# Gate and up projections of an FFN in one pass, two of eight k pairs with seven block products instead of eight

## The chip, the cores and the metric

The kernel runs on one core of a Trainium2 chip. The metric is the device time of one launch in microseconds, as the median over runs; the kernel before takes 2212.3 us (three runs, 2211.59 to 2212.45).

TensorE (PE) multiplies and adds up into PSUM; its weight loads are shown apart as PEld. VectorE is DVE, ScalarE is ACT, GpSimd is POOL, and SyncE (SP) issues the loads of weights from HBM.

## The reference, cut to what matters

Two residual layers on 256 tokens of width 2048: a mixer, then a dense SwiGLU FFN of inner width 5632, twice, then a final RMSNorm. The change touches the two FFNs alone.

```python
D_MODEL, SEQ, DEPTH = 2048, 256, 2
D_FF = 5632

def swiglu(x, wg, wu, wd):
    return (jax.nn.silu(x @ wg) * (x @ wu)) @ wd
...
h = h + swiglu(rms_norm(h, ffn_norm[layer]), ffn_w_gate[layer], ffn_w_up[layer], ffn_w_down[layer])
```

## The kernel before

All weights are float32 and each is used once. A product in float32 precision is made of three passes: a value is split into a rounded part `hi` (by ACT, `AF.Copy` into float32r) and the rest `lo` (by DVE, a subtraction), and `x @ w` becomes `xh@wh + xl@wh + xh@wl`. Activations are split once per layer, weights as they arrive.

**Streaming the weights.** `order` (L285) lists all weight blocks in the order of use. `load_next` (L71) issues the next 512 KB tile `w` (128 partitions x 1024) on SP's queue, into one of four buffers (`WBUFS`). `split_next` (L92) takes the oldest loaded tile, makes `wh` (ACT, L102) and `wl` (DVE, L103) of it, in one of three buffers each, puts its two halves (512 columns, one k tile each) on the list `pend`, and calls `load_next`, whose DMA must wait until the `w` tile four back has been read. `quarter` (L114) calls `fill`, which splits tiles until more than `ahead` = 3 halves are pending, lets delayed work run (`tick`), and hands out the oldest half.

**The FFN** (`ffn`, L431). The inner width is 11 blocks of 512 columns, in two groups (`HALVES`: 6 and 5 blocks). For each block `gemm_tok` (L200) makes the gate product in two PSUM banks (one for each 128 tokens): 16 k tiles, for each of them six matmuls 128x128 by 128x512. ACT reads it out with SiLU (`sg`, L444). Then `gemm_tok` makes the up product in two further banks, which DVE reads out and multiplies (`ac`, L449). Three quarters later (`self.later(3, turn)`) `turn` transposes `ac` on PE (L463, eight 128x128 transposes into two `sm` banks) and splits it into `hh` and `hl` (L166, L167). After a group's blocks, its down projection (L478) runs over `HX` for four blocks of output columns.

So a block of gate and up is 2 x 16 x 6 = 192 matmuls, 16 weight tiles and 8 transposes; there are 22 such blocks in the two FFNs. PSUM has four `mm` banks (gate and up of a block, used in turn) and four `sm` banks (transposes and small sums).

The order on each engine is set by the tile framework's scheduler, which may move independent instructions past each other; instructions on one engine run in that order, and each waits for semaphores of others.

Of the kernel before, what the change touches and what calls it, by code (L numbers as in the profile page):

```python
# [18 lines left out]
P = 128  # L19
T = 256  # L20
# [10 lines left out]
WBUFS = 4  # L31
WARM = 10
EARLY = 4
HALVES = ((0, 6), (6, NFB))
XPOS, APOS, SPOS = [(0, 1), (1, 0), (1, 2)], [(2, 0), (2, 1)], 1
GAPS = dict(
# [16 lines left out]
class Trunk:  # L53
# [17 lines left out]
    def load_next(self):  # L71

        if not self.blocks:
            return
        src = self.blocks[0]
# [11 lines left out]
        self.loaded.append(w)  # L87
        self.half = 0 if end else 1
        if end:
            self.blocks.pop(0)  # L90

    def split_next(self):  # L92

        nc = self.nc
        w = self.loaded.pop(0)
# [12 lines left out]
        self.load_next()  # L108

    def fill(self):  # L110
        while len(self.pend) <= self.ahead and self.loaded:
# [173 lines left out]
    def order(self):  # L285
        a, b = self.a, []
# [26 lines left out]
    def build(self):  # L313
        tc, nc, a = self.tc, self.nc, self.a
        self.ahead, self.half, self.early = 3, 0, EARLY
        self.blocks, self.loaded, self.pend = self.order(), [], []
        self.delayed, self.lane, self.wait = [], [], 0
        with (
            tc.tile_pool(name="const", bufs=1) as cp,
            tc.tile_pool(name="xs", bufs=4) as self.xs,  # L320
# [17 lines left out]
            with tc.tile_pool(name="even", bufs=1) as self.tp:  # L338
                X, ssq = self.even_mix()
            with tc.tile_pool(name="ff0", bufs=1) as self.tp:  # L340
                X, ssq = self.ffn(X, ssq, "g_od", self.rope_tables)
                rs = self.rstd_tok(ssq)
            with tc.tile_pool(name="odd", bufs=1) as self.tp:
                X, ssq = self.odd_mix(X, rs)
            with tc.tile_pool(name="ff1", bufs=1) as self.tp:
# [82 lines left out]
        nc.scalar.activation(rb, ps[:, :T], AF.Copy)  # L428


    def ffn(self, X, ssq, gname, between=None):  # L431
        nc = self.nc
        rs = self.rstd_tok(ssq)
        new_ssq = self.xs.tile([P, 2, 4], F32, tag="ssq", name="ssq", bufs=2)
        for half, (b0, b1) in enumerate(HALVES):
            HX = []
            if half and between:
                between()
            for b in range(b0, b1):
                pg = self.gemm_tok(X, range(4))  # L440
                sg, ac = [], []
                for t in range(2):
                    s = self.tp.tile([P, 512], F32, tag="sg", name="sg", bufs=2)
                    nc.scalar.activation(s, pg[t], AF.Silu, scale=rs[:, t : t + 1])  # L444
                    sg.append(s)
                pu = self.gemm_tok(X, range(4))
                for t in range(2):
                    s = self.tp.tile([P, 512], F32, tag="ac", name="ac", bufs=2)
                    nc.vector.scalar_tensor_tensor(  # L449
                        out=s, in0=pu[t], scalar=rs[:, t : t + 1], in1=sg[t],  # L450
                        op0=ALU.mult, op1=ALU.mult,
                    )
                    ac.append(s)
                hh = self.tp.tile([P, 4, T], F32R, tag="hh", name="hh", bufs=6)
                hl = self.tp.tile([P, 4, T], F32R, tag="hl", name="hl", bufs=6)
                HX += [(hh[:, j], hl[:, j]) for j in range(4)]
# [1041 lines left out]
```

## Time and profile before

| | |
|---|---|
| median of three runs | 2212.3 us |
| profiled execution: its own time, its span | 2212.2 us, 2210.4 us |
| PE busy | 2192.0 us, 99% of the span |
| DVE busy | 1291.7 us, 58% |
| ACT busy | 1051.7 us, 48% |
| DMA | mean 183 GB/s; 57.6% of 16 engines on the weight queue |

The profile is one execution. A busy PE counts overlapping matmuls (each row lasts some 390 ns while the next begins sooner), so its share says that PE is never without work, and the time of a matmul is to be read from the distance of starts. In the waits, ACT waits for PE to free a buffer and DVE waits for ACT: both are ahead of PE.

### The profile page before, as it was taken

The page shows a single profiled execution, that of the slowest core. Times are in us where ns is not written, and L with a number is a line of the kernel's source. Part 1 is how long each engine was busy: PE and PEld are TensorE (multiplying, and loading weights), DVE is VectorE, ACT ScalarE, POOL GpSimd, SP SyncE. Part 2 cuts the span into 40 slices and gives each one's busy share as a digit, 9 for nine tenths or more (in the row PEclk, how much of TensorE's full clock was granted, in tenths as well). Part 3 has the DMA queues.
Part 4 walks back from the last instruction along what each step waited for, and adds up shares of the span by engine and source line. Part 5 has one row for each costly group of instructions (what it writes and reads, how often), then busy time and mean ns, then how long its engine had stood idle before and what let it go on. Part 6 is the DMA issues. An engine that isn't in the chain of part 4 may idle for free.

```text
span 2210.4 us, 29062 instructions
## 1 busy us (share of the span) xinstructions
PE 2192.0 (99%) x11278; PEld 1826.9 (83%) x11278; DVE 1291.7 (58%) x1782; ACT 1051.7 (48%) x1435; POOL 30.0 (1%) x41
## 2 busy tenths in 40 slices
PE   9999999999999999999999999999999999999998
PEld 8888888778888888888888888888888888888886
DVE  6886688476454444444555688564454454444554
ACT  7755564464444433444444545454444433444443
POOL 0000100000000000000000000000000000000000
PEclk9999999999999999999999999999999999999999
DMA  8466347446666665666665554466665666666664
GB/s 294 143 187 181 120 144 227 144 136 200 190 189 189 190 193 192 191 190 191 190 188 185 179 162 143 150 201 189 190 190 188 190 194 193 192 191 190 188 191 154
DMA packets 124650, 405.14 MB, mean 183 GB/s; under 512 B 24896, under 2 KB 25152, under 8 KB 124128
## 3 DMA queue, kind: packets, MB, share of 16 engines
q1 hardware_dynamic: 122896, 398.31, 57.6%
q0 software_dynamic: 896, 3.80, 0.5%
q8 instruction: 88, 1.44, 0.3%
q10 hardware_dynamic: 720, 1.18, 0.1%
q14 instruction: 50, 0.41, 0.0%
HBM read 400.10 MB, written 3.15 MB: 182 GB/s over the span
## 4 chain that ended last, share of the span: by engine, by line
PE 92%; DVE 3%; ACT 2%; issue 1%; DMA 0%; POOLq 0%; POOL 0%; SPq 0%; DVEq 0%
PE mm L59 87%; PE sm L59 4%; DVE wl L103 1%; PE sm L463 1%; ACT wh L102 1%; PE sm L225 0%; DMA dN<-DG 0%; ACT DG L789 0%; DMA Nb<-dN 0%; PE sm L1303 0%; ACT TT L793 0%; DVE h L757 0%; DVE G L782 0%; ACT G L794 0%; DVE h L756 0%
## 5 line engine op out<-in xcount | busy, mean ns | idle before, releaser
L103 DVE TENSOR_TENSOR wl<-w,wh 128x1024 fp32r<-128x1024 f32 (+1 forms) x745 | 907.4, 1218 | 795.4 <-ACT wh L102 793.5
L102 ACT ACTIVATE wh<-w 128x1024 fp32r<-128x1024 f32 (+1 forms) x745 | 786.1, 1056 | 1001.9 <-PE mm L59 948.7
L59 PE MATMUL mm<-wh,x 128*128 128x512 f32 x3328 | 897.8, 391 | 0.9 <-DVE x L167 0.6
L59 PEld LDWEIGHTS mm<-wh,x 128*128 128x128 f32 x3328 | 620.3, 188 | 128.9 <-DVE x L167 0.9
L59 PE MATMUL mm<-wl,x 128*128 128x512 f32 x1664 | 513.6, 390 | 0.7 <-DVE wl L103 0.7
L59 PEld LDWEIGHTS mm<-wl,x 128*128 128x128 f32 x1664 | 312.2, 188 | 66.4 <-DVE wl L103 1.1
L59 PE MATMUL mm<-x,wh 128*128 128x512 f32 x992 | 357.4, 402 | 1.6 <-ACT wh L102 1.6
L59 PE MATMUL mm<-x,wl 128*128 128x256 f32 x992 | 279.7, 282 | 0.6 <-DVE wl L103 0.6
L59 PE MATMUL mm<-wh,hh 128*128 128x512 f32 x704 | 274.5, 390 | 0.0
L59 PE MATMUL mm<-wh,hl 128*128 128x512 f32 x704 | 273.9, 389 | 0.0
L59 PEld LDWEIGHTS mm<-x,wh 128*128 128x128 f32 x992 | 186.8, 188 | 45.2 <-ACT wh L102 1.8
L59 PE MATMUL mm<-wl,hh 128*128 128x512 f32 x704 | 220.1, 389 | 0.0
L59 PEld LDWEIGHTS mm<-x,wl 128*128 128x128 f32 x992 | 188.1, 190 | 2.0 <-DVE wl L103 1.6
L59 PEld LDWEIGHTS mm<-wl,hh 128*128 128x128 f32 x704 | 132.2, 188 | 27.4
L59 PEld LDWEIGHTS mm<-wh,hl 128*128 128x128 f32 x704 | 132.2, 188 | 27.3
L59 PEld LDWEIGHTS mm<-wh,hh 128*128 128x128 f32 x704 | 132.2, 188 | 27.1
L59 PE MATMUL mm<-l,wh 128*128 128x512 f32 x120 | 44.0, 404 | 0.0
L255 DVE TENSOR_TENSOR h<-mm,h 128x512 f32<-128x512 f32 x54 | 34.7, 685 | 11.6 <-PE mm L59 11.6
L449 DVE SCALAR_TENSOR_TENSOR ac<-mm,rstd,sg 128x512 f32<-128x512 f32 x44 | 31.0, 746 | 14.0 <-PE mm L59 14.0
L59 PE MATMUL mm<-l,wl 128*128 128x256 f32 x120 | 34.5, 288 | 0.0
L167 DVE TENSOR_TENSOR hl<-sm,hh 128x512 fp32r<-128x512 f32 x44 | 28.2, 682 | 0.0
L169 ACT ACTIVATE x<-sm,pkt 128x256 fp32r<-128x256 f32 x52 | 22.4, 470 | 10.8 <-DVE x L170 9.8
(260 smaller groups left out, 1078.4 us busy)
## 6 DMA issues: line engine op xcount, KB each, us to landing
w<-f_gate SPq DMA_DIRECT2D x176, 512.0 KB, 4.4
w<-f_up SPq DMA_DIRECT2D x176, 512.0 KB, 3.8
w<-f_down SPq DMA_DIRECT2D x176, 512.0 KB, 4.4
w<-e_in SPq DMA_DIRECT2D x94, 512.0 KB, 4.3
w<-e_out SPq DMA_DIRECT2D x32, 512.0 KB, 4.4
w<-o_out SPq DMA_DIRECT2D x32, 512.0 KB, 3.7
w<-o_in SPq DMA_DIRECT2D x26, 512.0 KB, 3.8
w<-e_in SPq DMA_DIRECT2D x16, 256.0 KB, 6.1
```

The lines of the kernel that those rows point to most:

```text
L59: return self.nc.tensor.matmul(out, lhsT, rhs, start=start, stop=stop, skip_group_check=shared)
L102: nc.scalar.activation(hi[:, sl], w[:, sl], AF.Copy)
L103: nc.vector.tensor_tensor(out=lo[:, sl], in0=w[:, sl], in1=hi[:, sl].bitcast(F32), op=ALU.subtract)
L167: nc.vector.tensor_tensor(out=lo, in0=src, in1=hi.bitcast(F32), op=ALU.subtract)
L169: nc.scalar.activation(hi, src, AF.Copy, scale=scale)
L255: nc.vector.tensor_tensor(out=hs, in0=ps[t], in1=hs, op=ALU.add)
L449: nc.vector.scalar_tensor_tensor(out=s, in0=pu[t], scalar=rs[:, t : t + 1], in1=sg[t], op0=ALU.mult, op1=ALU.mult,)
L463: nc.tensor.transpose(pt[:, i * T + t * P : i * T + t * P + P], ac[t][:, (j + i) * P : (j + i + 1) * P], self.ident,)
```

## The change

**Order of the products.** Gate and up of a block are made in one pass over k (`gate_up`) instead of one after the other, in four `mm` banks `c[n][t]` (n is gate or up, t the half of the tokens). k is taken in eight pairs of k tiles. In six pairs, each pair is one gate tile and one up tile of 1024 columns, as now, and takes eight block products of three matmuls, 24 matmuls.

**Seven products.** In pairs 3 and 7 (`SPAIRS`) the 2x2 block product (two token halves x two k tiles, by two k tiles x gate and up) is made by Strassen's algorithm in Winograd's form: seven products of three matmuls (`triple`), 21 matmuls for 24. One each goes to `c[0][0]`, `c[1][0]` and `c[0][1]`, and four into the `sm` banks `q[0]` to `q[3]`, which add up over both pairs.

**Sums of blocks.** Products need sums of blocks. On the side of the activations `x_sums` makes four sums for each of the two pairs once per FFN (DVE, and one split). On the side of the weights `split_pair` makes, for each such pair of tiles, four differences of 512 columns (DVE), and splits them in two steps of 1024 (ACT and DVE), beside the split of one block `b22`; the second half of the up tile is not split as it stands. The gate tile `w` is held until then, and its `load_next` is called together with that of the up tile.

**Reading out.** At a block's end ACT copies the four `mm` banks and `q[0]` to SBUF, and DVE makes eight sums and two products, with two SiLU on ACT between them (before: two SiLU and two products). `turn` comes nine quarters later (`TURN`) instead of three.

Nothing else is changed: the same bytes are loaded, and the mixers, down projections and the end are as they were.

```diff
+TURN = 9
+SPAIRS = (3, 7)
...
         hi = self.wp.tile([P, 1024], F32R, tag="wh", name="wh", bufs=3)
         lo = self.wp.tile([P, 1024], F32R, tag="wl", name="wl", bufs=3)
+        if role == "up":
+            self.split_pair(self.held, w, hi[:, 0:512], lo[:, 0:512])
+            self.load_next()
+            self.load_next()
+            return
...
-        self.load_next()
+        if role == "gate":
+            self.held = w
+        else:
+            self.load_next()
+
+    def split_pair(self, wg, wu, hi, lo):
+
+        V = self.nc.vector
+        b11, b21, b12, b22 = wg[:, 0:512], wg[:, 512:], wu[:, 0:512], wu[:, 512:]
+        self.split((hi, lo), b22)
+        t = self.tp.tile([P, 4, 512], F32, tag="o", name="t", bufs=self.tbufs)
+        th = self.tp.tile([P, 4, 512], F32R, tag="th", name="th")
+        tl = self.tp.tile([P, 4, 512], F32R, tag="tl", name="tl")
+        for o, x, y in (
+            (t[:, 0], b12, b11), (t[:, 1], b22, t[:, 0]), (t[:, 3], b21, t[:, 1]),
+            (t[:, 2], b22, b12),
+        ):
+            V.tensor_tensor(out=o, in0=x, in1=y, op=ALU.subtract)
+        for i in (2, 0):
+            self.split((th[:, i : i + 2], tl[:, i : i + 2]), t[:, i : i + 2])
+        self.pend.append(((hi, lo), *((th[:, i], tl[:, i]) for i in range(4))))
...
-                    r += [a["f_gate"][l, n, kc] for kc in range(4)]
-                    r += [a["f_up"][l, n, kc] for kc in range(4)]
+                    for p in range(8):
+                        cs = slice(p % 2 * 1024, p % 2 * 1024 + 1024)
+                        wg, wu = (a[k][l, n, p // 2][:, cs] for k in ("f_gate", "f_up"))
+                        r += [("gate", wg), ("up", wu)] if p in SPAIRS else [wg, wu]
...
+    def triple(self, out, x, w, start, stop):
+        self.mm(out, x[0], w[0], start, False)
+        self.mm(out, x[1], w[0], False, False)
+        self.mm(out, x[0], w[1], False, stop)
...
+        a11, a21, a12, a22 = x[:, 0, 0], x[:, 0, 1], x[:, 1, 0], x[:, 1, 1]
+        s = self.tp.tile([P, 4, P], F32, tag="e3", name="s")
+        V.tensor_tensor(out=s[:, 0], in0=a21, in1=a22, op=ALU.add)
+        V.tensor_tensor(out=s[:, 1], in0=s[:, 0], in1=a11, op=ALU.subtract)
+        V.tensor_tensor(out=s[:, 2], in0=a11, in1=a21, op=ALU.subtract)
+        V.tensor_tensor(out=s[:, 3], in0=a12, in1=s[:, 1], op=ALU.subtract)
+        self.split(dst, s)
...
+        c = [[self.ps("mm") for _ in range(2)] for _ in range(2)]
+        q = None
+        for p in range(8):
+            k = 2 * p
+            if p not in SPAIRS:
+                for n in range(2):
+                    for j in range(2):
+                        w = self.quarter()
+                        for t in range(2):
+                            end = n == 1 and t == 1 and j == 1 and p == LASTP
+                            self.triple(c[n][t], x(k + j, t), w, k + j == 0, end)
+                continue
+            b11, b21 = self.quarter(), self.quarter()
+            b22, t1, t2, t3, t4 = self.quarter()
+            new, end = q is None, p == SPAIRS[-1]
+            q = q or [self.ps() for _ in range(4)]
+            sh, sl = sums[p]
+            s1, s2, s3, s4 = ((sh[:, i], sl[:, i]) for i in range(4))
+            self.triple(c[0][0], x(k + 1, 0), b21, False, end)
+            self.triple(c[1][0], s4, b22, False, end)
+            self.triple(c[0][1], x(k + 1, 1), t4, False, end)
+            self.triple(q[0], x(k, 0), b11, new, end)
+            self.triple(q[1], s2, t2, new, end)
+            self.triple(q[2], s3, t3, new, end)
+            self.triple(q[3], s1, t1, new, end)
...
+        for o, i in ((u[1], c[1][1]), (g[0], c[0][0]), (u[0], c[1][0]), (g[1], c[0][1])):
+            S.activation(o, i, AF.Copy)
+        S.activation(u2, q[0], AF.Copy)
+        add(g[0], q[0], g[0])
+        S.activation(g[0], g[0], AF.Silu, scale=rs[:, 0:1])
+        add(u2, q[1], u2)
+        add(u3, q[2], u2)
+        add(g[1], g[1], u3)
+        S.activation(g[1], g[1], AF.Silu, scale=rs[:, 1:2])
+        for t, y in ((0, u2), (1, u3)):
+            add(u[t], q[3], u[t])
+            add(u[t], u[t], y)
+        for t in range(2):
+            V.scalar_tensor_tensor(
+                out=u[t], in0=u[t], scalar=rs[:, t : t + 1], in1=g[t],
+                op0=ALU.mult, op1=ALU.mult,
...
+            self.later(6 + 2 * i, lambda p=p: self.x_sums(X0, p, sums[p]))
...
-                pg = self.gemm_tok(X, range(4))
-                sg, ac = [], []
-                for t in range(2):
-                    s = self.tp.tile([P, 512], F32, tag="sg", name="sg", bufs=2)
-                    nc.scalar.activation(s, pg[t], AF.Silu, scale=rs[:, t : t + 1])
-                    sg.append(s)
-                pu = self.gemm_tok(X, range(4))
...
+                ac = self.gate_up(X, sums, rs)
...
-                self.later(3, turn)
+                self.later(TURN, turn)
```

Where the instructions stand, at the end of the third block of the first FFN and in the fourth. **DVE at the block's end, before**: the two products that read out the up banks (`ac`), two weight splits, and the splits of the transposed block (`hl`).

```order
L103 TENSOR_TENSOR wl_5967<-w_5898,wh_5966 128x1024
L103 TENSOR_TENSOR wl_5985<-w_5916,wh_5984 128x1024
L449 SCALAR_TENSOR_TENSOR ac_5996<-mm_5850,rstd_5045,sg_5846 128x512
L449 SCALAR_TENSOR_TENSOR ac_5998<-mm_5851,rstd_5045,sg_5848 128x512
L103 TENSOR_TENSOR wl_6011<-w_5934,wh_6010 128x1024
L103 TENSOR_TENSOR wl_6043<-w_5952,wh_6042 128x1024
L167 TENSOR_TENSOR hl_6001<-sm_6022,hh_6000 128x512
L167 TENSOR_TENSOR hl_6001<-sm_6029,hh_6000 128x512
L103 TENSOR_TENSOR wl_6061<-w_5970,wh_6060 128x1024
```

**DVE at the same place, after**: `eg`, `eu`, `eq`, `e3` are the SBUF tiles of the read-out, `sm` the four banks `q`; the `wl` rows are splits of tiles of the next block, the first two of its pair 0, then those of pair 1.

```order
L522 TENSOR_TENSOR eg0_6106<-sm_5929,eg0_6106 128x512
L522 TENSOR_TENSOR eq_6110<-sm_5930,eq_6110 128x512
L522 TENSOR_TENSOR eu0_6108<-sm_5932,eu0_6108 128x512
L522 TENSOR_TENSOR e3_6111<-sm_5931,eq_6110 128x512
L522 TENSOR_TENSOR eu0_6108<-eu0_6108,eq_6110 128x512
L522 TENSOR_TENSOR eg1_6107<-eg1_6107,e3_6111 128x512
L522 TENSOR_TENSOR eu1_6109<-sm_5932,eu1_6109 128x512
L536 SCALAR_TENSOR_TENSOR eu0_6108<-eu0_6108,rstd_5045,eg0_6106 128x512
L522 TENSOR_TENSOR eu1_6109<-eu1_6109,e3_6111 128x512
L113 TENSOR_TENSOR wl_6142<-w_6063,wh_6141 128x1024
L536 SCALAR_TENSOR_TENSOR eu1_6109<-eu1_6109,rstd_5045,eg1_6107 128x512
L113 TENSOR_TENSOR wl_6160<-w_6065,wh_6159 128x1024
```

Ten instructions of the read-out stand ahead of the second split of the next block's pair 1 (`wl_6160`), where two stood.

**DVE at pair 3 of that next block, after**: `t` holds the four differences, `tl` their `lo` parts, `wl_6244` is that of `b22`, `w_6145` and `w_6163` are the gate and the up tile of pair 3.

```order
L135 TENSOR_TENSOR t_6247<-w_6163,w_6145 128x512
L113 TENSOR_TENSOR wl_6228<-w_6145,wh_6227 128x1024
L197 TENSOR_TENSOR hl_6130<-sm_6207,hh_6129 128x512
L197 TENSOR_TENSOR hl_6130<-sm_6214,hh_6129 128x512
L135 TENSOR_TENSOR t_6247<-w_6163,t_6247 128x512
L197 TENSOR_TENSOR wl_6244<-w_6163,wh_6243 128x512
L135 TENSOR_TENSOR t_6247<-w_6145,t_6247 128x512
L135 TENSOR_TENSOR t_6247<-w_6163 128x512
L197 TENSOR_TENSOR tl_6249<-t_6247,th_6248 128x1024
L113 TENSOR_TENSOR wl_6269<-w_6181,wh_6268 128x1024
L197 TENSOR_TENSOR tl_6249<-t_6247,th_6248 128x1024
```

The first row needs the up tile `w_6163`, and the other rows stand behind it. The buffer of that tile is the one that `wl_6160` above reads, four tiles back. Before, a pair of tiles was two `wl` rows.

**PE in a block, before**: two banks in turn, `wh` twice and `wl` once for each; here from one k tile to the next.

```order
L59 MATMUL mm_5370<-wl_5379,x_4812 128x512
L59 MATMUL mm_5371<-wl_5379,x_4812 128x512
L59 MATMUL mm_5370<-wh_5410,x_4812 128x512 x2
L59 MATMUL mm_5371<-wh_5410,x_4812 128x512 x2
L59 MATMUL mm_5370<-wl_5411,x_4812 128x512
L59 MATMUL mm_5371<-wl_5411,x_4812 128x512
```

**PE at pair 3 of the next block, after**: `sh3` and `sl3` are the sums of activations, `th` and `tl` the split differences; two matmuls with `wh_6227` stand just ahead.

```order
L62 MATMUL mm_6131<-wl_6228,x_4812 128x512
L62 MATMUL mm_6133<-wh_6243,sh3_5049 128x512
L62 MATMUL mm_6133<-wh_6243,sl3_5050 128x512
L62 MATMUL mm_6133<-wl_6244,sh3_5049 128x512
L62 MATMUL sm_6280<-wh_6227,x_4812 128x512 x2
L62 MATMUL sm_6280<-wl_6228,x_4812 128x512
L62 MATMUL mm_6132<-th_6248,x_4812 128x512 x2
L62 MATMUL sm_6281<-th_6248,sh3_5049 128x512
L62 MATMUL sm_6281<-th_6248,sl3_5050 128x512
L62 MATMUL sm_6281<-tl_6249,sh3_5049 128x512
L62 MATMUL sm_6282<-th_6248,sh3_5049 128x512
L62 MATMUL mm_6132<-tl_6249,x_4812 128x512
```

The last row is the third matmul of the product with the fourth difference; it stands behind fifteen matmuls of the pair (the two just ahead and the thirteen here), and five more follow it. Each waits on what DVE and ACT make for this pair; before, only on `wh` and `wl`.

## Rows read from the trace of the kernel before

**Rows 1.** The page: span, and busy time of each engine.

```profile
span 2210.4 us, 29062 instructions
PE 2192.0 (99%) x11278; PEld 1826.9 (83%) x11278; DVE 1291.7 (58%) x1782; ACT 1051.7 (48%) x1435; POOL 30.0 (1%) x41
```

**Rows 2.** The chain of work, 470 to 560 us: start us, us, what.

```profile
483.69 43.54 PE mm L59 x192
527.23 0.87 PE sm L463 x8
528.10 31.98 PE mm L59 x141
```

**Rows 3.** PE's timeline in a block: start us, us, engine, line, operation, out<-in, count.

```profile
597.76 0.62 PE L59 MATMUL mm<-wl,x 128*128 128x512 f32 x2
598.21 1.07 PE L59 MATMUL mm<-wh,x 128*128 128x512 f32 x4
599.12 0.62 PE L59 MATMUL mm<-wl,x 128*128 128x512 f32 x2
599.57 1.07 PE L59 MATMUL mm<-wh,x 128*128 128x512 f32 x4
```

**Rows 4.** Waits of the run: who for whom, us in total, times, longest us.

```profile
ACT wh L102 <- PE mm L59: 948.7, 615, 4.2
DVE wl L103 <- ACT wh L102: 793.5, 574, 4.8
```

**Rows 5.** Groups by shape: busy us, mean ns of one, idle before.

```profile
L103 DVE TENSOR_TENSOR wl<-w,wh 128x1024 fp32r<-128x1024 f32 x737 | 902.0, 1224 | 794.2 <-ACT wh L102 792.3 <-PE sm L59 0.8 <-PE mm L59 0.5
L102 ACT ACTIVATE wh<-w 128x1024 fp32r<-128x1024 f32 x737 | 781.2, 1060 | 1000.6 <-PE mm L59 948.7 <-issue 35.3 <-DMA w<-e_out 4.0
L255 DVE TENSOR_TENSOR h<-mm,h 128x512 f32<-128x512 f32 x54 | 34.7, 685 | 11.6 <-PE mm L59 11.6
L449 DVE SCALAR_TENSOR_TENSOR ac<-mm,rstd,sg 128x512 f32<-128x512 f32 x44 | 31.0, 746 | 14.0 <-PE mm L59 14.0
L444 ACT ACTIVATE sg<-mm,rstd 128x512 f32<-128x512 f32 x44 | 27.5, 674 | 0.0
L167 DVE TENSOR_TENSOR x<-mix,x 128x512 fp32r<-128x512 f32 x7 | 4.8, 684 | 0.1
L769 ACT ACTIVATE BKt<-sm 128x512 f32<-128x512 f32 x8 | 4.7, 588 | 3.2 <-PE sm L766 3.2
```

**Rows 6.** Busy time in stretches: us, PE, PEld, DVE, ACT, POOL, PEclk, DMA share, GB/s.

```profile
482.00:526.00 44.00, 44.00 (x200) 36.53 (x199) 35.01 (x66) 22.02 (x27) 2.35 (x2) 1.00 0.62 187
526.00:570.00 44.00, 44.00 (x200) 36.53 (x199) 21.80 (x20) 19.11 (x20) 0.00 (x0) 1.00 0.62 190
1474.00:1518.00 44.00, 44.00 (x200) 36.54 (x199) 22.31 (x24) 22.02 (x27) 1.30 (x2) 1.00 0.65 214
```

**Rows 7.** DVE's timeline around a read-out, columns as in 3.

```profile
613.14 1.41 DVE L449 SCALAR_TENSOR_TENSOR ac<-mm,rstd,sg 128x512 f32<-128x512 f32 x2 [0.63 <-PE mm L59]
614.47 1.22 DVE L103 TENSOR_TENSOR wl<-w,wh 128x1024 fp32r<-128x1024 f32 x1
616.73 1.23 DVE L103 TENSOR_TENSOR wl<-w,wh 128x1024 fp32r<-128x1024 f32 x1 [1.04 <-ACT wh L102]
617.87 1.28 DVE L167 TENSOR_TENSOR hl<-sm,hh 128x512 fp32r<-128x512 f32 x2
```

**Rows 8.** ACT's timeline around a read-out.

```profile
546.74 1.06 ACT L102 ACTIVATE wh<-w 128x1024 fp32r<-128x1024 f32 x1 [1.66 <-PE mm L59]
547.71 1.25 ACT L444 ACTIVATE sg<-mm,rstd 128x512 f32<-128x512 f32 x2
549.46 1.06 ACT L102 ACTIVATE wh<-w 128x1024 fp32r<-128x1024 f32 x1 [0.51 <-PE mm L59]
```

**Rows 9.** The page's DMA issues: line, operation, count, KB each, us to landing.

```profile
w<-f_gate SPq DMA_DIRECT2D x176, 512.0 KB, 4.4
w<-f_up SPq DMA_DIRECT2D x176, 512.0 KB, 3.8
```

More of the change, by code (lines that the diff above doesn't have):

```diff
@@ L33 @@
 EARLY = 4
+TURN = 9
+SPAIRS = (3, 7)
+LASTP = max(p for p in range(8) if p not in SPAIRS)
 HALVES = ((0, 6), (6, NFB))
@@ L74, in load_next @@
             return
-        src = self.blocks[0]
+        src, role = self.blocks[0], None
+        if isinstance(src, tuple):
+            role, src = src
         w = self.wp.tile([P, 1024], F32, tag="w", name="w", bufs=WBUFS)
@@ L86, in load_next @@
             end = o + 1024 == src.shape[-1]
-        self.loaded.append(w)
+        self.loaded.append((w, role))
         self.half = 0 if end else 1
@@ L94, in split_next @@
         nc = self.nc
-        w = self.loaded.pop(0)
+        w, role = self.loaded.pop(0)
         hi = self.wp.tile([P, 1024], F32R, tag="wh", name="wh", bufs=3)
         lo = self.wp.tile([P, 1024], F32R, tag="wl", name="wl", bufs=3)
+        if role == "up":
[3 more added lines that the diff above has]
+            return
         n = 512 if self.early else 1024
@@ L317, in build @@
         self.delayed, self.lane, self.wait = [], [], 0
+        self.tbufs = 1
         with (
@@ L344, in build @@
                 X, ssq = self.odd_mix(X, rs)
+            self.tbufs = 2
             with tc.tile_pool(name="ff1", bufs=1) as self.tp:
@@ L428, in row_bcast, with x_sums @@
         nc.scalar.activation(rb, ps[:, :T], AF.Copy)
+    def triple(self, out, x, w, start, stop):
+        self.mm(out, x[0], w[0], start, False)
+        self.mm(out, x[1], w[0], False, False)
+        self.mm(out, x[0], w[1], False, stop)
+    def x_sums(self, X, p, dst):
+        V = self.nc.vector
+        x = self.tp.tile([P, 2, 2, P], F32, tag="eq", name="x")
+        for j in range(2):
+            xh, xl = X[2 * p + j][:2]
+            V.tensor_tensor(
+                out=x[:, j].rearrange("p t n -> p (t n)"), in0=xh.bitcast(F32),
+                in1=xl.bitcast(F32), op=ALU.add,
+            )
+        a11, a21, a12, a22 = x[:, 0, 0], x[:, 0, 1], x[:, 1, 0], x[:, 1, 1]
[5 more added lines that the diff above has]
+        self.split(dst, s)
@@ new lines, in gate_up @@
+    def gate_up(self, X, sums, rs):
+        nc, V, S = self.nc, self.nc.vector, self.nc.scalar
+        half = (slice(0, P), slice(P, T))
+        x = lambda k, t: (X[k][0][:, half[t]], X[k][1][:, half[t]])
+        c = [[self.ps("mm") for _ in range(2)] for _ in range(2)]
[4 more added lines that the diff above has]
+                for n in range(2):
+                    for j in range(2):
+                        w = self.quarter()
[16 more added lines that the diff above has]
+            self.triple(q[3], s1, t1, new, end)
+        e = lambda tag: self.tp.tile([P, 512], F32, tag=tag, name=tag)
+        g = [e("eg0"), e("eg1")]
+        u = [e("eu0"), e("eu1")]
+        u2, u3 = e("eq"), e("e3")
+        add = lambda o, i0, i1: V.tensor_tensor(out=o, in0=i0, in1=i1, op=ALU.add)
+        for o, i in ((u[1], c[1][1]), (g[0], c[0][0]), (u[0], c[1][0]), (g[1], c[0][1])):
[14 more added lines that the diff above has]
+                op0=ALU.mult, op1=ALU.mult,
+            )
+        return u
@@ L433, in ffn @@
         rs = self.rstd_tok(ssq)
+        sums = {}
+        for i, p in enumerate(SPAIRS):
+            sums[p] = tuple(
+                self.tp.tile([P, 4, P], F32R, tag=f"s{n}{p}", name=f"s{n}{p}") for n in "hl"
+            )
+            self.later(6 + 2 * i, lambda p=p: self.x_sums(X0, p, sums[p]))
+        X0 = X
         new_ssq = self.xs.tile([P, 2, 4], F32, tag="ssq", name="ssq", bufs=2)
@@ L439, in ffn @@
             for b in range(b0, b1):
-                pg = self.gemm_tok(X, range(4))
-                sg, ac = [], []
-                for t in range(2):
-                    s = self.tp.tile([P, 512], F32, tag="sg", name="sg", bufs=2)
-                    nc.scalar.activation(s, pg[t], AF.Silu, scale=rs[:, t : t + 1])
-                    sg.append(s)
-                pu = self.gemm_tok(X, range(4))
[L447 to L453, printed above, removed]
+                ac = self.gate_up(X, sums, rs)
                 hh = self.tp.tile([P, 4, T], F32R, tag="hh", name="hh", bufs=6)
```

## The prediction

> **What bounds the kernel now.** The page says that PE is busy for 99% of the span while DVE is at 58% and ACT at 48% [rows 1]. That share alone does not say that a matmul less saves its time, so the chain of work comes next: through a block of gate and up it is PE alone, 192 matmuls of line 59 in 43.54 us and the eight transposes in 0.87 us, with nothing between [rows 2]. So a matmul costs 43.54/192 = 0.2268 us; the timeline has the same distance (eight starts from 597.76 to 599.57, 0.226 apart) [rows 3], while a row itself lasts longer, as matmuls overlap. The waits show who has room: ACT waits for PE to free a buffer, DVE for ACT [rows 4]. In a block DVE works 21.8 of 44 us and ACT 19.1 [rows 6]. PE's order sets the end, and DVE and ACT are a few tiles ahead of it.
>
> **What is removed.** A pair with seven products has 21 matmuls for 24. Two pairs a block and 22 blocks take away 2 x 3 x 22 = 132 matmuls of 0.2268 us, 29.9 us. All of it lies on the path. A block then has 186 matmuls, 42.18 us, and with the transposes 43.05.
>
> **What DVE and ACT get.** In front of a pair with seven products stood one split of the up tile (1.22 us on DVE); now five instructions of 512 columns (0.684) and two of 1024 (1.224), 5.87 us, so 4.65 more, 9.3 a block. The read-out was two products of 0.746; now it is eight sums of 0.685 and the two products, 5.5 more [rows 5]. DVE goes from 21.8 to 36.6 us in 43.05. ACT gets two splits of 1.06 and one of 0.62 for one of 1.06 (3.4 a block, 0.62 by the longer form of 512 columns) and five copies of 0.588 [rows 5], and goes from 19.1 to some 25.4. Neither becomes the bound on the average. But DVE's work is bunched: the read-out at a block's end, and the eleven rows at pair 3.
>
> **How fast DVE gets through a bunch** decides. A DVE instruction that waits for nothing starts before the one ahead has ended: `wl` starts at 616.73, lasts 1.23, and `hl` starts at 617.87, 0.09 earlier than that end; the two `hl` together take 1.28 [rows 7], where one is 0.68. So in a bunch 1024 columns cost 1.14, 512 columns 0.60, and the product with a scalar 0.66 (two in 1.41) [rows 7]. ACT likewise: a split starts at 546.74 and the next instruction at 547.71, 0.97 later, and two SiLU take 1.25 [rows 8], so 0.97 for 1024 columns and 0.49 for a copy of 512.
>
> The Trainium skill (VectorE: DVE Perf Modes, § The DRAIN you can't avoid) says that the next operation does not start until the pipe of the one before is empty, and that chaining cannot skip this; its next section lets an instruction that isn't held start earlier. Here the trace speaks for the second: 0.08 to 0.09 us of overlap wherever nothing is waited for. By the first the sum would be that of the third rival below.
>
> **The chain through one block.** I count from the first matmul of a block, at 0.
> ACT can split the block's first tile when the tiles of the former pair 6 are free, at the start of pair 7: -21 x 0.2268 = -4.76. Then in its row come a split, a copy, a split and four copies, 0.97 + 0.49 + 0.97 + 3 x 0.49 + 0.59 = 4.49, so the copy that DVE's first sum needs ends at -0.27, and DVE starts at about -0.2.
> DVE goes through the rows up to `wl_6160`: eight sums at 0.60, a product 0.66, `wl_6142` 1.14, a product 0.66, `wl_6160` 1.22: 8.48, to 8.3. This frees the buffer for the up tile of pair 3.
> Its load lands 3.8 us later by the row of `f_up`, 4.4 by that of `f_gate` [rows 9]. I take the middle, 4.1, since both loads run on one queue and here come in closer succession than the 2.72 us between two splits now [rows 8]. It lands at 12.4.
> DVE then does its rows at pair 3: 0.60, 1.14, 2 x 0.60, 4 x 0.60, 1.14, 1.14, 1.22, together 8.84. The last `tl` is there at 21.2.
> PE wants it after 12 quarters of six matmuls (16.33), the transposes (0.87) and 15 matmuls of the pair (3.40): at 20.6. So PE waits 0.6 us, in each of the 18 blocks that follow another one in their group. With the landing between 3.8 and 4.4 it is 0.3 to 0.9.
> Pair 7 has no read-out ahead of it: from pair 3 to it DVE has three pairs' time, 16 us, for some 7 us of splits. I cost its wait at nothing. The transposes come nine quarters after the block's end, 12.2 us, and DVE has made the last product at 7.1; nothing again. The four `q` banks are read before 5 us, and the next block first wants one at 17; nothing. The `mm` banks are copied from -3.8 on and the second bank is wanted at 0.7: nothing, as long as ACT's row holds; the copies end at -0.8.
>
> **The entry of each FFN.** `x_sums` costs per pair two additions of 256 columns, four of 128 and a split of 512. From 512 to 1024 columns a DVE row grows by 0.54 us [rows 5], so 0.41, 0.28 and 0.68: 2.6, and 5.2 for both pairs. In the first block of the second FFN DVE had 22.3 us of work [rows 6]; 37 in 43 leaves it a wait of about 1, between 0 and 2. In the first block of the first FFN it had 35.0 [rows 6], because the rotary tables are made there; with 9.3 and 5.2 it is 49.5 in 43 by durations, some 7 less by the overlap of about 85 rows. So between 0 and 8 us are lost there; I take 4. Together 5.
>
> **The sum.** -29.9 + 18 x 0.6 + 5 = -14.1. The profiled execution takes 2212.2 (its span 2210.4 and 1.8 around it), the median of the runs 2212.3, so they can be taken as one: 2198.
>
> **Rivals.**
> *No wait at all.* The load lands sooner, in 3.4 or so, or DVE's rows come earlier than I count, and 0.6 us vanish from a chain of 21. For it: nothing waits in a block now [rows 2]. Against it: 29.9 is then all, with the entry at 0 to 5: 2182 to 2187.
> *Nothing to be seen.* The chain is 0.4 to 0.8 longer: loads that come in pairs land in 4.6 to 4.9. Then 18 waits of 1.0 to 1.4 and the entry give 2206 to 2213. The same mechanism as mine, with another size.
> *DVE is late, and the kernel slower.* Place: the rows from the first sum to the last `tl`. If they don't overlap, because each waits for the one ahead or for a semaphore, 20 of them cost 0.083 more, 1.7 us. Then 18 x 2.3 + 10 = 51 and the time is 2233. It decides from 1.4 us of wait a block (18 x 1.4 + 5 = 29.9). Against it: independent rows overlap [rows 7], and in the order rows that need each other mostly stand apart.
> *The products aren't cheaper.* If the 21 matmuls of such a pair, which change bank after two or three and read six tiles, went at 0.259, nothing would be saved, and with the waits it is 2228. Against it: the distance is the same for `wh` and `wl` rows now, which change bank after one and two [rows 3].
>
> **How the numbers follow.** Forecast with its own range of 2188 to 2207: 0.40. No wait: 0.20. Nothing to be seen: 0.18. Late DVE: 0.17. Products not cheaper: 0.05. A measurement of this kernel can tell about 0.2%, 4.4 us, from no change. Faster than that (below 2207.9) are the first two, 0.60; within it the third, 0.18; slower the last two, 0.22. The range takes in the full gain at its lower end; above, it leaves out the last two cases, which stand at 2228 and 2233, and reaches to 2222, half way from the third case to them.
>
> **What would show it.** Right: 186 matmuls in a block at 0.227; a block every 43.6 to 43.7 us against 44.41; one PE wait a block, for a DVE `tl` at pair 3, of 0.6 us, behind a DVE wait for the load of `f_up`; DVE rows of the read-out 0.60 apart. Wrong: a PE wait for `wl` at a block's start or at pair 7 (DVE late everywhere), distances of more than 0.23 in a pair with seven products, or no PE wait in a block.

## The result

The changed kernel takes 2228.4 us (median of 3 runs, 2227.8 to 2230.4) against 2212.3 (2211.6 to 2212.5): a ratio of 1.0075, with an interval of 1.0061 to 1.0089. It is 16 us slower, where 14 us faster was forecast, and above the range. The profiled execution is the median one, 2228.4 us with a span of 2226.6. (A correction to the section on the change: the half of the up tile that is not split as it stands is the first one, `b12`; the second, `b22`, is split.)

The page of after, beside [rows 1]:

```profile
span 2226.6 us, 29559 instructions
PE 2177.3 (98%) x11146; PEld 1795.5 (81%) x11146; DVE 1574.5 (71%) x2250; ACT 1166.0 (52%) x1637; POOL 29.1 (1%) x41
```

The 132 matmuls are gone (11278 before), yet PE's busy time fell by 14.7 us only and the span grew by 16.2: the saving of 29.9 us is lost and 16.2 more, 46.1 in all. Of these PE stands still for 30.9 us more than before; the other 15.2 lie in pauses too, but are counted as busy, since a matmul's row lasts 0.39 us where the next could start after 0.227, and the row behind a pause lasts longer (0.50). Where PE waits, the chain of work through one steady block tells (start us, us, what; "..." marks rows left out); in [rows 2] it was PE alone:

```profile
614.88 8.07 PE mm L62 x36
622.95 0.02 SPq L90
...
623.00 5.62 DMA w<-f_up
...
628.72 0.06 DVE t L135
...
629.33 0.15 DVE wl L113
...
630.47 1.28 DVE hl L197 x2
...
634.29 1.04 ACT th L196
...
636.34 1.23 DVE tl L197
...
637.61 0.50 PE mm L62
638.11 1.15 PE sm L62 x5
639.26 18.38 PE mm L62 x81
657.64 2.72 PE sm L62 x12
660.37 1.81 PE mm L62 x8
```

The block starts at 614.88 and the next one at 660.37, 45.5 us later; before, a block took 44.41. The matmuls keep their distance: 18.38/81 and 2.72/12 are 0.227. What is new is the detour in the middle: a load of pair 3's up tile, DVE's rows behind it, and PE taking up the last `tl` at 637.61. PE's timeline in that place (start, us, engine, line, operation, out<-in, count, and in brackets the idle time and who ended it) has two pauses, the longer one for ACT's `th`:

```profile
635.39 0.73 PE L62 MATMUL mm<-th,x 128*128 128x512 f32 x2 [1.20 <-ACT th L196]
...
637.61 0.50 PE L62 MATMUL mm<-tl,x 128*128 128x512 f32 x1 [0.57 <-DVE tl L197]
```

And over the whole run (engine, line, for whom: us in total, times, longest), where [rows 4] had no PE wait to show (DVE's 43 waits are those at pair 7 too, PE's are almost all at pair 3):

```profile
DVE t L135 <- DMA w<-f_up: 88.6, 43, 3.8
PEld mm L62 <- ACT th L196: 27.0, 18, 1.6
PEld mm L62 <- DVE tl L197: 19.7, 20, 1.3
```

DVE's timeline of the block shows the read-out and what follows it:

```profile
614.46 0.69 DVE L522 TENSOR_TENSOR eg<-sm,eg 128x512 f32<-128x512 f32 x1 [0.73 <-ACT eq L525]
615.07 0.68 DVE L522 TENSOR_TENSOR eq<-sm,eq 128x512 f32<-128x512 f32 x1
...
621.72 2.35 DVE L113 TENSOR_TENSOR wl<-w,wh 128x1024 fp32r<-128x1024 f32 x2
...
628.72 0.69 DVE L135 TENSOR_TENSOR t<-w 128x512 f32<-128x512 f32 x1 [3.25 <-DMA w<-f_up]
```

The read-out holds the splits up to 624, these free the buffers late, and so four loads go out in 4.3 us (SyncE's queue), where before a split every 2.72 us released one:

```profile
621.20 0.33 SPq L90 DMA_DIRECT2D w<-f_gate  x1
623.00 0.33 SPq L90 DMA_DIRECT2D w<-f_up  x1
624.10 0.33 SPq L90 DMA_DIRECT2D w<-f_gate  x1
625.50 0.33 SPq L90 DMA_DIRECT2D w<-f_up  x1
```

The second of them is pair 3's up tile. DVE then stands for 3.25 us in front of the first difference, the row that needs it.

Over the run, the starts of that load in the chain give a block of 45.34 us on the average (nine blocks between 623.00 and 2070.72), 2.29 above the 43.05 that PE's rows alone make. 18 x 2.29 = 41 us of the 46 between 2212.3 - 29.9 = 2182.4 and the time measured. At the entries of the FFNs PE's timeline shows two pauses, in the first FFN early in its second block and in the second FFN at its first pair 3:

```profile
530.18 0.73 PE L62 MATMUL mm<-wl,x 128*128 128x512 f32 x2 [0.60 <-DVE wl L113]
...
1501.95 0.50 PE L62 MATMUL mm<-tl,x 128*128 128x512 f32 x1 [0.87 <-DVE tl L197]
```

By the distance of PE's starts beyond 0.227 they cost 0.9 and 1.1 us. So the waits at pair 3 and the entries make 43 of the 46; the rest was not followed.

### The profile page after: what moved, and what is told of

It reads as the page before. It is cut to its first block, busy times and chain, and to the rows that moved or that the text cites. A ratio compares the mean times of both kernels' runs of the same rounds, so it can differ in the third digit from the quotient of the medians.

```text
span 2226.6 us, 29559 instructions
## 1 busy us (share of the span) xinstructions
PE 2177.3 (98%) x11146; PEld 1795.5 (81%) x11146; DVE 1574.5 (71%) x2250; ACT 1166.0 (52%) x1637; POOL 29.1 (1%) x41
## 4 chain that ended last, share of the span: by engine, by line
PE 80%; DVE 7%; ACT 4%; DMA 4%; issue 3%; SPq 0%; POOLq 0%; POOL 0%; DVEq 0%
PE mm L62 71%; PE sm L62 8%; DMA w<-f_up 3%; ACT wh L112 2%; DVE wl L113 2%; DVE tl L197 1%; DVE hl L197 1%; ACT th L196 1%; DVE t L135 1%; PE sm L255 0%; PE sm L568 0%; DMA dN<-DG 0%; ACT DG L894 0%; DMA Nb<-dN 0%; DVE ou L934 0%
## 5 line engine op out<-in xcount | busy, mean ns | idle before, releaser
L113 DVE TENSOR_TENSOR wl<-w,wh 128x1024 fp32r<-128x1024 f32 (+1 forms) x701 | 849.3, 1216 | 441.2 <-ACT wh L112 438.8
L62 PE MATMUL mm<-wh,x 128*128 128x512 f32 x2712 | 820.0, 392 | 0.8 <-DVE x L197 0.5
L62 PEld LDWEIGHTS mm<-wh,x 128*128 128x128 f32 x2712 | 504.7, 188 | 105.4 <-DVE x L197 0.9
L62 PEld LDWEIGHTS mm<-wl,x 128*128 128x128 f32 x1356 | 253.1, 188 | 57.2 <-DVE wl L113 5.0
L135 DVE TENSOR_TENSOR t<-w 128x512 f32<-128x512 f32 x88 | 58.6, 689 | 88.6 <-DMA w<-f_up 88.6
L196 ACT ACTIVATE th<-t 128x1024 fp32r<-128x1024 f32 x88 | 90.3, 1052 | 54.1 <-DVE t L135 54.0
L197 DVE TENSOR_TENSOR tl<-t,th 128x1024 fp32r<-128x1024 f32 x88 | 105.2, 1218 | 0.0
L135 DVE TENSOR_TENSOR t<-w,t 128x512 f32<-128x512 f32 x88 | 60.4, 686 | 0.8
L62 PE MATMUL sm<-th,sh 128*128 128x512 f32 x132 | 51.7, 391 | 0.0
L62 PE MATMUL sm<-th,sl 128*128 128x512 f32 x132 | 51.6, 391 | 0.0
```

What stands on the lines that cost most here:

```text
L62: return self.nc.tensor.matmul(out, lhsT, rhs, start=start, stop=stop, skip_group_check=shared)
L113: nc.vector.tensor_tensor(out=lo[:, sl], in0=w[:, sl], in1=hi[:, sl].bitcast(F32), op=ALU.subtract)
L135: V.tensor_tensor(out=o, in0=x, in1=y, op=ALU.subtract)
L196: nc.scalar.activation(hi, src, AF.Copy)
L197: nc.vector.tensor_tensor(out=lo, in0=src, in1=hi.bitcast(F32), op=ALU.subtract)
```

## The experiments

Theory L: pair 3's up load lands late behind the read-out, and everything else is as computed. Its rivals: D, the work on DVE itself (read-out and differences) is too much wherever it stands; P, the products cost what they did, whatever is loaded when. All ratios below are to runs of the kernel before on the same chip (2212.4 to 2212.5 us).

**Own buffers for the pairs' tiles.** The gate and up tile of a pair no longer take a buffer that a split of the pair before must free.

```
+        if role == "gate":
+            self.duo = self.tp.tile([P, 2, 1024], F32, tag="o", name="duo", bufs=2)
+            w = self.duo[:, 0]
+        elif role == "up":
+            w = self.duo[:, 1]
+        else:
+            w = self.wp.tile([P, 1024], F32, tag="w", name="w", bufs=WBUFS)
...
-        self.tbufs = 1
+        self.tbufs = 2
```

> The gate and the up tile of a pair with seven products get a buffer of their own (an 8 KB tile for both, in turn with the tile of the differences), so the load of pair 3's up tile no longer waits for the split of pair 1's up tile behind the read-out. All products, splits and sums stay. Theory L (the load of pair 3's up tile starts late, behind the read-out, and lands late, 5.6 us): the DVE wait for this load ends, the pair's rows can start at 10.6 instead of 13.7 after the block's start, the last tl comes at 19.5 before PE wants it at 20.6; a block takes 43.1 to 43.3 us instead of 45.5, and the time is 2228 - 18 x 2.3 = 2187, between 2183 and 2195. Rival D (DVE simply has too many rows between the read-out and pair 3): the wait moves to other rows and at least half of it stays: 2208 or more. Rival P (the products of a pair take longer than 0.227 us each): unchanged, 2228.

Measured: 2192.3 us (2190.6 to 2194.8), ratio 0.991 (0.9895 to 0.9925). With all of the arithmetic of the changed kernel it is 36 us faster than that, so D and P fall. The chain in the second FFN is PE alone again:

```profile
1510.05 10.93 PE mm L62 x48
1520.98 0.87 PE sm L574 x8
1521.85 7.50 PE mm L62 x33
...
1553.15 10.93 PE mm L62 x48
```

This block takes 43.10 us, without a wait. The load itself lands no sooner: the one for pair 3 of the block at 1553.15 takes 7.7 us, but it goes out at 1539.54, 13.6 us ahead of the block. Some 10 us stay lost against 2182.4. PE stops at the entry of the first FFN (last section), and in both FFNs DVE's order puts the first difference, with its wait for the load, ahead of the read-out, so that a split at the block's start comes late in some blocks (those of the second FFN take 43.05 to 44.2 us). In the first FFN (DVE's timeline, then PE's):

```profile
612.22 1.29 DVE L141 TENSOR_TENSOR t<-duo 128x512 f32<-128x512 f32 x2 [1.89 <-DMA duo<-f_up]
...
617.03 0.68 DVE L528 TENSOR_TENSOR eg<-sm,eg 128x512 f32<-128x512 f32 x1
```

```profile
623.77 0.74 PE L62 MATMUL mm<-wl,x 128*128 128x512 f32 x2 [0.55 <-DVE wl L119]
```

**Pair 7 alone, and pairs 4 and 7.** One line each: `SPAIRS = (7,)`, so that the read-out stays and pair 3 is an ordinary pair; and `SPAIRS = (4, 7)`, one pair further from the read-out.

> Only pair 7 is made with seven products: 66 matmuls less than the kernel before instead of 132, 15.0 us; the joint pass over eight banks and the long read-out stay, pair 3 has no differences. Theory L: no load is waited for at pair 3, the read-out alone costs PE next to nothing: 2212.3 - 15.0 + 2 = 2199, between 2196 and 2204. Rival R (the read-out with its ten DVE rows and the four copies holds PE at a block's start): over 2212, since then the wait is there with one pair too.

> Pairs 4 and 7 instead of 3 and 7 are made with seven products; the work is the same, the buffers are as in the changed kernel. The up tile of pair 4 takes the buffer that the split of pair 2's up tile frees, 2.7 us later than that of pair 1, but PE wants the pair 5.4 us later, and the splits of the transposed block are no longer among its rows (1.2 us). Theory L: rows done at 10.6 + 5.6 + 7.6 = 23.8 against 26.0 wanted: no wait at pair 4, 2228 - 41 = 2187, up to 2200 if pair 7 now waits for a load of its own. Rival D: 36.6 us of DVE work in a block as before, so 2215 to 2228. Rival P: 2228.

Measured: 2202.8 us (2202.2 to 2204.0), ratio 0.9957 (0.9942 to 0.9972), for pair 7 alone; 2207.4 (2203.0 to 2212.4), 0.9981 (0.9971 to 0.999), for 4 and 7. The read-out by itself thus costs nearly nothing, as L has it; but the block with pair 7 alone takes 44.1 us (611.47 to 655.58 in its chain) where 189 matmuls and the transposes make 43.7, and over the run PE loses 5.4 us at pair 7 by the distance of its starts, mostly in front of the split of `b22`, so pair 7 has a small wait of its own. With 4 and 7 that wait is in the chain of the second FFN, and it is for the split of `b22`:

```profile
1949.71 0.52 DVE tl L197
1950.23 0.61 DVE wl L197
...
1950.89 1.21 PE mm L62 x4
1952.10 2.75 PE sm L62 x12
```

The four and twelve matmuls are the last pair's. One pair's time more of room took away half of the loss, no more: 2187 was missed by 20 us. At pair 4 PE waits in a few blocks only, as L has it; by the distance of its starts some 18 of the 23 us by which the profiled execution stands above 2182.4 are at pair 7.

**What makes the load late?** First try: a 64-byte transfer out of pair 3's up tile was written behind its load, to hold the next loads back.

```
+        if role == "up" and self.mark_next:
+            self.nc.sync.dma_start(out=self.mark, in_=w[0:1, 0:16])
```

> As the changed kernel, but behind the load of pair 3's up tile SP issues a transfer of 64 bytes out of that tile, so that the next loads on SP's queue, which follow it after 1.1 and 2.5 us in the changed kernel, start only once it has landed. It still starts late, behind the read-out. Theory L in its second part (it lands in 5.6 us instead of 4.1 because the loads behind it share the DMA engines): the landing falls to 4.4 to 4.8, a block by 0.8 to 1.2 us, the time by 14 to 22 us, to 2206 to 2214, if the tiles of pair 4, which come later, are still in time. If the landing is long for another reason (the load ahead of it by 1.8 us alone): 5.2 or more and 2222 to 2232.

Measured: 2227.7 us (2226.3 to 2228.1), ratio 1.0068 (1.0053 to 1.0083). This decides nothing: the scheduler put the transfer behind the two loads that it was to hold (they go out at 624.46 and 625.87, it at 629.72), and the bunch stayed as it was. Second try, with the transfer writing into the buffer of the next tile, so that this tile's load must stand behind it:

```
+        if self.mark is not None:
+            self.nc.sync.dma_start(out=w[0:1, 0:16], in_=self.mark[0:1, 0:16])
+            self.mark = None
+        if role == "up":
+            self.mark, self.third = (w if self.third else None), not self.third
```

> Nothing of the computation changes: a 64-byte transfer out of pair 3's up tile into the next tile's buffer stands in SyncE's queue ahead of that tile's load, so that no load is issued between pair 3's up load and its landing. Theory B (the up load takes 5.1 to 5.9 us because loads are issued 1 to 2.5 us behind it): it lands after 4.1 to 4.6 us, VectorE's rows start 1.0 to 1.5 us earlier and the wait of a block falls from 2.1 to 0.6 to 1.1 us: 2228 - 18 x 1.0 to 1.5 = 2201 to 2210. Theory A (it is long because of the gate load 1.8 us ahead of it, or for itself): it still lands after 5.1 to 5.9 us, 2222 to 2230. If the loads held back are then late for pair 4 or 5, 2232 or more, and the landing alone decides between A and B.

Measured: 2215.7 us (2213.3 to 2217.6), ratio 1.0015 (1.0006 to 1.0025), 12.7 us less than the changed kernel. Now the loads behind are held (issue times of SyncE), and the landing is shorter (chain):

```profile
623.40 0.33 SPq L95 DMA_DIRECT2D w<-f_up  x1
628.33 0.50 SPq L84 DMA_DIRECT2D w<-w  x1
```

```profile
623.40 4.87 DMA w<-f_up
...
668.18 4.55 DMA w<-f_up
```

In 16 blocks of its chain that load takes 4.55 to 4.97 us; in the changed kernel's it takes 5.14 to 6.15. So the loads issued 1 to 2.5 us behind it cost it some 0.7 us: theory B, but for half of the excess over 4.1. The other half remains when nothing is issued behind it, and the gate load 1.8 us ahead need not be its cause: in the changed kernel's first block of each FFN's second group that load goes out 2.62 us behind the gate load and 2.72 ahead of the next (885.54, 888.16, 890.88; 1886.18, 1888.80, 1891.52), and still takes as long (view of the DMA issues for each of these two loads):

```profile
w<-f_up SPq DMA_DIRECT2D x1, 512.0 KB, 4.7
...
w<-f_up SPq DMA_DIRECT2D x1, 512.0 KB, 4.6
```

In the kernel before, with loads 2.72 us apart, single ones took 3.4 to 4.8 us (529 to 605 us in its trace): mostly 4.2 to 4.8 up to 574, 3.4 to 3.9 behind it, gate and up alike. So 4.1 is the middle between two levels, and what sets the level no run shows. The gain is 0.7 us a block (12.7/18). It may be put down to the landing, though that is not shown apart, since the scheduler's order shifted as well: DVE's rows up to the last `tl` are 1.0 us shorter there (both `tl` stand together), and PE wants that `tl` five matmuls, 1.1 us, earlier, so that the two about cancel.

**What stands behind the late load?** In VectorE's order at pair 3 (in the section on the change) the first difference, which needs the up tile, stands ahead of three rows that don't: the split of the gate tile and the two splits of the transposes (`hl`), 1.14 + 1.28 us. The chain above has all of them behind the load. A fourth, the split of a tile of pair 4 (1.14 us), stands between the two `tl`. A copy of one element from the gate tile's `lo` into `t`, which the difference overwrites, puts the difference behind the three, and with it no other row stands between the two `tl`:

```
+        V.tensor_copy(out=t[0:1, 0, 0:1], in_=self.heldlo.bitcast(F32)[0:1, 0:1])
```

> Same loads, same buffers, same arithmetic; only VectorE's order at pair 3 changes: the gate tile's own split (1.14 us) and the two splits of the read-out's transposes (1.28 us) stand ahead of the first difference that needs the up tile, and nothing stands between the two `tl` rows (1.14 us more). Theory (the 2.1 us wait of a block is the load's landing plus 8.85 us of VectorE rows behind it): after the landing some 6.4 us of rows are left, last `tl` 13.8 to 14.1 us after the up load's issue less 2.4, so before PE wants it at +20.6; the wait goes from 2.1 to 0 to 0.4 us a block, 2228.4 - 18 x 1.9 = 2194 us (2188 to 2202). Rival (the load is late and whatever stands behind it shifts with it, so that the wait comes back at pair 4, whose splits now stand behind both `tl`): 2205 to 2216. Rival (the wait is TensorE's own or the load's alone, VectorE's order does not matter): 2226 to 2230.

Measured: 2204.3 us (2203.2 to 2206.5), ratio 0.9964 (0.9952 to 0.9977): 24 us less than the changed kernel with the same loads, buffers and sums, so VectorE's order matters and the third reading falls; but 2 us above the range of the theory, and the wait comes back in another place, though not at pair 4. At pair 3 PE's timeline shows no idle time any more (at `th` a start stands 0.39 us behind the one before, so some 0.3 are left); at pair 7 the same copy puts the differences behind the gate tile's split, and PE is held there (chain):

```profile
647.46 1.24 DVE wl L113
...
651.52 2.36 DVE tl L198 x2
...
653.93 0.50 PE mm L62
```

From 610.12 to 653.93 a block takes 43.8 us. So the copy was made at pair 3 alone (for both differences that read the up tile first):

```
+        if self.nth % len(SPAIRS) == 0:
+            V.tensor_copy(out=t[0:1, 0:3:2, 0], in_=self.heldlo.bitcast(F32)[0:1, 0:2])
+        self.nth += 1
```

> The order of e5_gate_first at pair 3 alone; at pair 7 VectorE's order is that of the changed kernel again. Theory: what e5 lost after the pair 3 wait was gone is its own doing at pair 7 (the differences there stood behind the gate tile's split, block period 43.8 us where TensorE's rows alone make 43.05): without it 2204 - 18 x 0.7 = 2191 us (2187 to 2198), period 43.05 to 43.3. Rival (moving the rows at pair 3 pushes other splits late, and pair 7's wait comes from that): 2200 to 2207, period 43.6 or more.

Measured: 2199.3 us (2196.3 to 2201.7), ratio 0.9941 (0.9926 to 0.9956). The order at pair 3 alone is worth 29 us. The blocks still take 43.5 to 44.0 (43.8 on the average from 1553.74 to 1728.90), which is the rival's sign. Pair 7 has a wait, for the split of `b22` behind a DVE wait for the load (DVE's timeline, then PE's):

```profile
1544.73 1.29 DVE L138 TENSOR_TENSOR t<-w 128x512 f32<-128x512 f32 x2 [2.91 <-DMA w<-f_up]
...
1551.81 0.68 DVE L200 TENSOR_TENSOR wl<-w,wh 128x512 fp32r<-128x512 f32 x1
```

```profile
1552.55 0.50 PE L62 MATMUL mm<-wl,sh 128*128 128x512 f32 x1 [0.85 <-DVE wl L200]
```

By the distance of PE's starts, 8.7 of the 18.5 us by which the profiled execution stands above 2182.4 are at pair 7, in most blocks less than here, and 5.2 at pair 3, at `th`. With pair 7 alone it was 5.4 at pair 7, with no rows of pair 3 to push anything; so most of this wait is pair 7's own, and the rest may be the rival's.

Then the split of `b22` was put ahead of the last two differences at both pairs, by a copy from its `lo` into `t`:

```
+        V.tensor_copy(out=t[0:1, 1, 0:1], in_=lo.bitcast(F32)[0:1, 0:1])
```

> The order of e9 at pair 3, and at both pairs the split of b22 (`wl`, 0.60 us) ahead of the last two differences, where e9 had it behind both `tl` rows at pair 7 and TensorE waited up to 0.85 us a block for it. Theory (the wait at pair 7 is this row, and was covered before by the longer wait at pair 3): period 43.05 to 43.3 us, 2199 less 18 x 0.3 to 0.7 = 2187 to 2194. Rival (at pair 7 the rows behind the load are a chain whichever comes first, so that the last `tl` is late instead, and at pair 3 one split of another tile falls back between the differences and `tl`): 2196 to 2204.

Measured: 2201.6 us (2200.2 to 2202.6), ratio 0.9949 (0.9933 to 0.9966); the rival. PE no longer waits for `wl`, but for `th` of the same pair, and the block takes 43.87 (1553.36 to 1597.23):

```profile
1553.09 0.23 ACT th L200
...
1553.36 0.73 PE mm L62 x2
```

At pair 7 the rows behind the load are one chain, and their order only says which of them is last. What is left there is the load; that own buffers take it away fits the first run above, where PE's timeline has no pause at pair 7.

**Both together, and three pairs.** Own buffers with the first copy (the order at both pairs); then pairs 3, 5 and 7 with own buffers: with that order (at every pair), with none, and with the order at pair 3 alone.

```
-SPAIRS = (3, 7)
+SPAIRS = (3, 5, 7)
...
-        junk = self.tp.tile([P, 512], F32, tag="junk", name="junk", bufs=1)
+        junk = self.tp.tile([P, 512], F32, tag="e3" if self.alt else "junk", name="junk", bufs=1)
```

> Own buffers for the pairs' gate and up tiles and VectorE's order of the other run together. With own buffers no wait is left in a block of the second FFN; what is left of e1_own_buffers' 10 us above 2182 stands at the first FFN's first blocks, where the first `tl` waits for VectorE. Theory: the order saves up to 2.4 us there once or a few times: 2186 to 2192. Rival (the entry is bound by the loads, not by the order): 2191 to 2195.

> As the run ahead of it, with three pairs of eight (3, 5, 7) by seven products for eight; the square's throw-away output shares a buffer so that the tiles fit. TensorE loses 66 more matmuls of 0.2268 us, 15.0 us in all. Theory: where own buffers hold, 2188 - 15 = 2173 (2170 to 2182). Rival (VectorE, 71% busy, gets 8.3 us of rows more a block, of which pair 5's differences wait behind pair 3's, and two buffers for three pairs tie pair 7's load to pair 3's splits): a wait of 1 us or more a block, 2190 to 2210.

> Three pairs (3, 5, 7) with own buffers, VectorE's order as the scheduler sets it. Theory: e1_own_buffers' 2192 less 66 x 0.2268 = 15.0 us: 2177 (2173 to 2184). Rival (the scheduler puts the first difference of pair 3 ahead of the read-out, so that the load's wait holds the read-out and the next pairs' splits in most blocks, where e1 had it in the first ones only): 2190 to 2205.

> As e10_three_own, with the order of e9 at pair 3 of each block alone. Theory: the read-out no longer stands behind the wait for pair 3's load and pairs 5 and 7 keep their order: 2170 to 2178. Rival (as e8_three_pairs, whose losses were at the first FFN's entry and not from the order): 2186 to 2190.

Measured: own buffers with the order at both pairs 2206.2 us (2205.1 to 2209.5), 0.9973 (0.9962 to 0.9985), a miss by 14 us and on the other side: the order harms at pair 7 here as it did above (`wl` 605.20, `tl` 609.25, PE at 611.67), and own buffers alone were better. Three pairs: 2188.7 (2187.6 to 2189.9), 0.9893 (0.9878 to 0.9908), with the order at every pair; 2192.0 (2190.2 to 2193.2), 0.9908 (0.9893 to 0.9923), with none; 2186.4 (2185.7 to 2187.6), 0.9885 (0.9868 to 0.9901), with the order at pair 3 alone. All three stand 7 to 8 us above the ranges of their theories. Without an order two buffers bind three pairs, and the up load, which goes out right behind the split of an earlier pair's `b22` (it ends at 1536.99), is in the steady chain again:

```profile
1537.38 6.66 DMA duo<-f_up
...
1550.25 0.50 PE mm L62
```

From 1550.25 to 1594.00 a block takes 43.75 us for PE's 42.37 (43.05 less three matmuls); over the run it is 42.5 to 45.6. With the order at pair 3 the block is down to 42.72 (the transposes start at 1518.76 and 1561.48); at the first FFN's entry PE works 40.9 and 42.6 us in the two stretches of 44 us from 482 on. These two make some 11 of the 19 us between this kernel and 2182.4 - 15.0; the rest was not followed. This last kernel is the best of the study, 1.15% faster than the kernel before and 1.9% faster than the changed one.

## Why the prediction was wrong

Its chain through a block was the right one, link by link, and one term of it, too small, turned the gain into a loss; two others were off by less.

- *Removed: 132 matmuls of 0.2268 us, 29.9 us.* Right. The rival by which the products would not be cheaper is refuted: 0.227 in and out of a pair, and the block of the run with own buffers takes 43.10 us where 43.05 was computed.
- *DVE's first sum at -0.2, the split that frees the buffer done at 8.3.* Measured -0.4 and 8.1 (614.46 and 622.95 against 614.88).
- *The load lands after 4.1 us, between 3.8 and 4.4.* **This step failed.** It took 5.6 in the block shown and 5.1 to 6.2 in the chain's blocks, so 1.0 to 2.1 longer than the value taken. The two medians of [rows 9] were those of a kernel in which the loads go out 2.72 us apart; the prediction said itself that here they come closer together, and yet kept the upper row as the end of its range. In the block shown 1.5 us were missing. Some 0.7 of them come from the loads issued behind it; the rest is there without them, since single loads took up to 4.8 already in the kernel before, which its medians hide. With 5.6 in the place of 4.1 the prediction's own sum gives a wait of 2.1. The rival "nothing to be seen" had the mechanism ("loads that come in pairs land in 4.6 to 4.9"), again with too small a size; what lands in 4.6 to 5.0 is the load with nothing issued behind it.
- *DVE's rows from there to the last `tl`, 8.84 us.* Measured 8.85 (628.72 to 637.57). The size was right and its reading was not: 1.14 + 1.28 us of these rows didn't need the load, and stood behind it only by the scheduler's order, and 1.14 more stood between the two `tl`. With these rows out of the way at pair 3 the kernel gains 29 us. The prediction took the order for a cost.
- *PE wants it at 20.6 and waits 0.6.* PE had it at 22.7 (637.61), so it lost 2.1; a little more went with the stops: the first matmul behind one is followed by the next after 0.34 and not 0.227. On the average of the blocks it is 2.3, 41 us for 18, where 10.8 stood.
- *The entries, 5 us (4 in the first FFN, 1 in the second).* Too much: 0.9 and 1.1 by PE's pauses there. This error went the other way, and the forecast would have been 3 us further off without it.
- *Pair 7, transposes, banks: nothing.* Right for the transposes and banks. Pair 7 does have a wait, of 0.2 to 0.4 us a block on the average, with one pair (5.4 us in 22 blocks) and with pair 3's wait gone (8.7); in the changed kernel, where the longer wait stands ahead, PE hardly waits there.
- *Products not cheaper, 2228.* The measured time to the microsecond, by luck: the distance in a pair is 0.227, and not the 0.259 that this rival needs.
- *Late DVE, 2233.* Near the time, and with the very wait of 2.3 a block, by the wrong cause. DVE's rows overlap as forecast: 0.60 apart where one lasts 0.68, in the read-out too. The Trainium skill (VectorE: DVE Perf Modes, § The DRAIN you can't avoid) says that the next op does not start until the pipe is empty, but that one that is not held starts earlier; these rows agree with the second.

The signs named beforehand were the right ones to look at, and came true in part: PE waits at pair 3, behind DVE's wait for the load of `f_up`, but in two pauses, the longer one for ACT's `th` (1.20 us) and one for `tl` (0.57), and it loses 2.3 in the place of 0.6.

## What to carry to other kernels

A load's time to land, taken from a row of the kernel before, holds only for the spacing of loads in that row: where a change bunches the releases of buffers, it has to be priced from loads that are issued as close together, or bounded far above the median; and a median can lie between two levels that single loads show. When an in-order engine waits for a load, read which of the rows behind it need that load; those that don't can go ahead of it, and here that order at pair 3 was worth 29 us, as much as the saved matmuls. Removing the longest wait uncovers the next one (pair 7's here), so a gain from a fix is bounded by both. A load that lands late does no harm if it goes out early enough: with own buffers it took 7.7 us in a block in which PE waited for nothing.

## What the hardware showed that was not expected

- A 512 KB load on SyncE's queue took 5.1 to 6.2 us with loads issued 1.8 us ahead and 1.1 and 2.5 us behind it, 4.55 to 4.97 with none behind it until it had landed, against medians of 3.8 and 4.4, and single times of 3.4 to 4.8 (those of 529 to 605 us), in the kernel before, where loads go out 2.72 us apart.
- In the run with own buffers PE stopped twice at the entry of the first FFN, for 1.19 and 0.71 us, and the granted clock fell behind it (columns: stretch, us, PE busy, count, clock, DMA share, GB/s):

```profile
498.00:504.00 6.00, 3.99 (x15) 0.96 0.45 143
504.00:508.00 4.00, 4.00 (x13) 0.63 0.88 267
```

  For some 3 us matmuls stood 0.43 apart (starts at 504.79, 505.22, 505.64), near twice 0.227: the lower of the two levels, 1.2 GHz for 2.4. After pauses of 1.20 and 0.57 us in the changed kernel's steady block the distance stayed at 0.23. What makes the difference, no run shows.
